# Seven-phase fp32 network: norm sums on VectorE, the norm's factor spread by a product with the identity, gate product and some weight parts on VectorE

## The chip, the cores and the metric

The kernel runs on one core of one Trainium2 chip. The metric is the device time of one execution in microseconds; lower is better. The reference's inputs are 512 tokens of width 1024 (and 256 memory tokens), everything in fp32.

## The reference, cut to what matters

Seven residual phases follow each other. Each starts with a root-mean-square norm, whose sum runs over the 1024 features of a token:

```
rmsnorm(x, g) = x * rsqrt(mean(x*x, axis=-1) + eps) * g
h  = x + mixer(rmsnorm(x))                 # mix: gated state-space part (inner norm "ssd") and pooling part
h += memory_attention(rmsnorm(h), rmsnorm(mem))   # xattn: 4 heads, 256 memory tokens
h += (silu(gate) * up) @ w_down            # ffn: gate, up = rmsnorm(h) @ w_gate_up, 2 x 2816 wide
h  = rmsnorm(h)                            # end of the first block ("end")
h += stick_breaking_attention(rmsnorm(h))  # stick ("begin"): 16 heads
h += relu(rmsnorm(h) @ w1)**2 @ w2         # mlp1: 4096 wide
h += nsa_attention(rmsnorm(h))             # nsa: compressed, selected and window attention, shared K and V
h += relu(rmsnorm(h) @ w1)**2 @ w2         # mlp2
out = rmsnorm(h)                           # "final"
```

## The kernel before, in words

**Layout.** Activations lie feature-major: `h` is 8 k-tiles of 128 features by 512 tokens. A projection yields one 128x512 PSUM bank per output tile, a *group*. fp32 products are put together from two parts of each operand, a rounded high part and the remainder: `group` (L556) issues, for each k-tile, the matmuls `wh*xh`, `wh*xl`, `wl*xh`. So a group over eight k-tiles is 24 matmuls of 128x128 weights by 512 tokens, one over six k-tiles 18.

**Weights.** `Weights` (L303) goes through one list of pieces (mostly 128x1024) in the order of use. For each piece, SP loads it into `ws` (3 buffers), ScalarE copies the rounded part `wh` (L341), and the remainder `wl` = `ws` - `wh` is a subtraction (L350): on GpSimd for the 14 pieces named in the set `POOL_LO` (L29), on VectorE for all others. `get` (L363) makes pieces two ahead of the one that it returns, inside the instruction stream of whatever asks for it; `no0`, the attention's output projection, asks for three ahead (L2003). Pieces of the second projection in feed-forward's last block are 768 wide (six k-tiles).

**Norms.** `Norm.tile` (L382) is called for each of the eight k-tiles as it becomes final. ScalarE squares it (L385 for the first, straight into `acc`; L388 into `sq`, two buffers, for the others), and GpSimd adds the square into `acc` (L392, seven times a norm, six for "final", half the width for the memory). `ssq` (L426) is a product with a column of ones that brings the token sums onto partitions, and a few small VectorE and ScalarE instructions (L412) that give the factor `tm`, 128 tokens by 4 columns. `bcast` (L429) spreads this factor over all 128 partitions: for each of the four columns VectorE multiplies the identity by the column (`dg`, two buffers, L436), TensorE multiplies a matrix of ones by it (L437), and VectorE copies the 128x512 result out of PSUM (`r`, L439). `Norm2` (L444), between the two blocks, keeps two norms, "end" and "begin", fed from the same tiles, and spreads two factors.

**Who calls them.** `proj` (L565) runs three lead groups, the sums (`ssq`), a fourth group, then `bcast`, and evacuates the groups with the spread factor afterwards. Evacuations of the mixer's pooling projection, `ev_pool` (L811), place the sums and broadcasts of "ssd" (m = 4, 5) and of the memory (m = 6, 7) between groups, behind VectorE's addition into `h` (L812). `feed` (L631) is the end of a residual phase: VectorE adds the group to `h` (L628), then `Norm.tile`, then the split into `xh` on ScalarE (L552) and `xl` on VectorE (L553) for the next phase; weight remainders of the next groups come between tiles. At the end of feed-forward (L1311 on) `ev` does this for eight tiles and feeds both norms of `Norm2`. `g_z` (L787) gates the mixer's output tile by tile and feeds the norm "ssd" in the midst of the state-space work. In feed-forward's first projections `ev` (L1279) scales each group by the factor (L1281); for even groups ScalarE takes the Silu (L1283), for odd ones GpSimd multiplies by the gate (L1286, 22 times), and the product is split.

**Order.** The scheduling is manual: each engine runs its instructions in the order in which the program issues them, so an instruction that waits holds all later ones of its engine. SP issues the weight loads, ScalarE some others. Generators in `bg` are advanced by `tick` between groups.

Of the kernel before, what the change touches and what calls it, by code (L numbers as in the profile page):

```python
# [10 lines left out]
F32 = mybir.dt.float32  # L11
# [3 lines left out]
ALU = mybir.AluOpType  # L15
# [3 lines left out]
P = 128  # L19
# [6 lines left out]
NEG = -1e30  # L26
CMP_FIRST = {1: (0,), 2: (1,), 3: (2, 3)}
CMP_AT = (1, 2, 4, 5)
POOL_LO = {"xs3", "xs5", "C1", "v1", "v4", "v6", "v7", "mk3", "xq6", "nc01", "nk10", "cw0.1", "nq3",  # L29
           "no3"}  # L30
PHASES = ("mix", "xattn", "ffn", "stick", "mlp1", "nsa", "mlp2")
BANKS = {"b": range(8), "bp": [0], "bo": [1], "za": [2, 3], "zb": [4, 6],
         "s": [0, 1, 2], "t": [3, 4, 5, 6], "av": [7], "f": [0, 1, 2, 3]}
# [269 lines left out]
class Weights:  # L303
# [42 lines left out]
    def lo(self):  # L346
        while self.half:
            i, s, n, hi, lo = self.half.popleft()
            e = self.nc.gpsimd if self.pieces[i][0] in POOL_LO else self.nc.vector
            e.tensor_tensor(lo[:, :n], s, hi[:, :n].bitcast(F32), op=ALU.subtract)  # L350
# [20 lines left out]
class Norm:  # L371
# [10 lines left out]
    def tile(self, src, scale=1.0):  # L382
        nc = self.s.nc
        if self.count == 0:
            nc.scalar.activation(self.acc, src, AF.Square, scale=scale)  # L385
        else:
            q = self.s.keep.tile([P, T], F32, name=f"sq_{self.name}{self.count}", tag="sq", bufs=2)
            nc.scalar.activation(q[:, :self.n], src, AF.Square, scale=scale)  # L388
            if self.count == KT - 1 and self.apart:
                self.rest = q  # L390
            else:
                nc.gpsimd.tensor_tensor(self.acc, self.acc, q[:, :self.n], op=ALU.add)  # L392
        self.count += 1

    def mean(self, src=None, more=None):
# [33 lines left out]
    def bcast(self, tm=None, tag="rbc", bufs=2):  # L429

        s, nc = self.s, self.s.nc
        tm = self.tm if tm is None else tm
        ps = s.bank()
        for i in range(self.n // P):
            dg = s.keep.tile([P, P], F32, name=f"dg_{self.name}{i}", tag="dg", bufs=2)
            nc.vector.tensor_scalar(dg, s.ident, tm[:, i:i + 1], None, op0=ALU.mult)  # L436
            nc.tensor.matmul(ps[:, P * i:P * i + P], s.ones, dg, start=True, stop=True)  # L437
        r = s.keep.tile([P, T], F32, name=f"r_{self.name}", tag=tag, bufs=bufs)[:, :self.n]
        nc.vector.tensor_copy(r, ps[:, :self.n])  # L439
        self.bc = r  # L440
        return r
# [26 lines left out]
class Kernel:  # L468
# [799 lines left out]
    def _ffn(self):  # L1268
        nc = self.nc
        norm, (xh, xl) = self.norm, self.x  # L1270
        hid = [self.newx(), (self.tmp("hh", (P, KT, T), F32R, bufs=1),
                             self.tmp("hl", (P, KT, T), F32R, bufs=1))]
        gate = {}

        def up(b, norm_):
            j0, j1 = FF_BLOCKS[b]
            hh, hl = hid[b % 2]

            def ev(i, ps):  # L1279
                t = self.tmp("t", bufs=4)  # L1280
                nc.vector.tensor_tensor(t, ps, norm.bc, op=ALU.mult)  # L1281
                if i % 2 == 0:
                    nc.scalar.activation(t, t, AF.Silu)  # L1283
                    gate[0] = t
                else:
                    nc.gpsimd.tensor_tensor(t, t, gate[0], op=ALU.mult)  # L1286
                    self.split(hh[:, i // 2, :], hl[:, i // 2, :], t)

            self.proj([f"f{a}{j}" for j in range(j0, j1) for a in "gu"], xh, xl, ev, norm=norm_)

        def down(b, ev):
            j0, j1 = FF_BLOCKS[b]
            self.proj([f"fd{b}.{m}" for m in range(8)], *hid[b % 2], ev, nk=j1 - j0)

        def plain(m, ps):
            nc.vector.tensor_tensor(self.h[:, m, :], self.h[:, m, :], ps, op=ALU.add)

        up(0, norm)
        up(1, None)
        down(0, plain)  # L1300
        up(2, None)
        down(1, plain)
        if self.nxt == "stick":
            nxt, nx = Norm2(self), self.newx()
            gf = self.col("final_norm")
            both = self.keep.tile([P, KT], F32, name="gboth")
            nc.vector.tensor_tensor(both, gf, self.next_gain, op=ALU.mult)
            nc.scalar.preload_act_table_set("natural_log_exp_and_others")

            def ev(m, ps):  # L1310
                self.resid(m, ps, nxt, both, nx)  # L1311
                nxt.second.tile(self.h[:, m, :], gf[:, m:m + 1])
        else:
            nxt, nx = None, None

            def ev(m, ps):
                plain(m, ps)
        down(2, ev)
        self.norm, self.x = nxt, nx
# [899 lines left out]
```

## Time and profile before

| | |
|---|---|
| median of three runs | 2227.06 us (2223.79 to 2227.17) |
| the profiled execution | 2227.83 us |
| its span, first to last instruction | 2226.0 us |
| mean granted TensorE clock | 0.990 |
| VectorE, ScalarE busy in the span | 55%, 39% |

The profile is that of one execution. A time in a row is microseconds unless marked ns; a stretch A:B counts from the span's start. Busy times are summed per engine; "PE" is TensorE's matmuls, "PEld" its weight loads, DVE is VectorE, ACT is ScalarE, POOL is GpSimd. An instruction is named by its line in the kernel, its engine, its operation and the tiles it writes and reads. An arrow (`<-DVE wl L350`) names what the engine waited for: the idle time before the instruction ended when that one did.

### The profile page before, as it was taken

The page shows a single profiled execution, that of the slowest core. Times are in us where ns is not written, and L with a number is a line of the kernel's source. Part 1 is how long each engine was busy: PE and PEld are TensorE (multiplying, and loading weights), DVE is VectorE, ACT ScalarE, POOL GpSimd, SP SyncE. Part 2 cuts the span into 40 slices and gives each one's busy share as a digit, 9 for nine tenths or more (in the row PEclk, how much of TensorE's full clock was granted, in tenths as well). Part 3 has the DMA queues.
Part 4 walks back from the last instruction along what each step waited for, and adds up shares of the span by engine and source line. Part 5 has one row for each costly group of instructions (what it writes and reads, how often), then busy time and mean ns, then how long its engine had stood idle before and what let it go on. Part 6 is the DMA issues. An engine that isn't in the chain of part 4 may idle for free.

```text
span 2226.0 us, 26742 instructions
## 1 busy us (share of the span) xinstructions
PE 2141.3 (96%) x10250; PEld 1735.1 (78%) x10250; DVE 1217.6 (55%) x1965; ACT 875.5 (39%) x1405; POOL 410.2 (18%) x429
## 2 busy tenths in 40 slices
PE   8899999999999999999899999999988899999998
PEld 5687888888888887877678888888766668888886
DVE  6988656554333336567655343445767745534333
ACT  4334434343222224355534332334547643523222
POOL 3433401011110104122210000012137631000001
PEclk9999999999999999999999999999999999999999
DMA  4222434122333223322132333324330113333231
GB/s 139 69 66 82 142 106 152 57 75 94 97 102 96 95 84 106 114 76 67 57 115 94 104 95 95 102 88 133 127 100 22 30 43 119 105 95 104 95 95 66
DMA packets 63375, 205.93 MB, mean 93 GB/s; under 512 B 7952, under 2 KB 8336, under 8 KB 63120
## 3 DMA queue, kind: packets, MB, share of 16 engines
q1 hardware_dynamic: 59504, 196.86, 28.2%
q10 hardware_dynamic: 3744, 7.37, 0.9%
q8 instruction: 80, 1.31, 0.2%
q14 instruction: 47, 0.39, 0.1%
HBM read 189.39 MB, written 6.29 MB: 88 GB/s over the span
## 4 chain that ended last, share of the span: by engine, by line
PE 77%; DVE 11%; ACT 5%; POOL 3%; issue 3%; DMA 1%; ACTq 0%; SPq 0%; POOLq 0%; DVEq 0%
PE psum L540 60%; PE b L540 15%; DVE wl L350 2%; POOL sph L1685 1%; ACT sT L1667 1%; ACT sT L1668 1%; PE psum L2092 1%; DVE t L908 1%; DVE spl L1690 1%; DVE xl L553 1%; DVE np L2070 1%; DVE sT L1662 1%; ACT xh L552 1%; DMA nq<-nq 1%; DVE pv L1089 0%
## 5 line engine op out<-in xcount | busy, mean ns | idle before, releaser
L540 PE MATMUL psum<-xh,wh 128*128 128x512 f32 x1560 | 610.8, 392 | 1.6 <-DVE h L628 0.9
L540 PE MATMUL psum<-xh,wl 128*128 128x512 f32 x1560 | 608.4, 390 | 3.2 <-DVE wl L350 3.0
L540 PE MATMUL psum<-xl,wh 128*128 128x512 f32 x1560 | 607.8, 390 | 0.0
L341 ACT ACTIVATE wh<-ws 128x1024 fp32r<-128x1024 f32 (+1 forms) x346 | 356.5, 1038 | 376.5 <-PE psum L540 312.8
L350 DVE TENSOR_TENSOR wl<-ws,wh 128x1024 fp32r<-128x1024 f32 (+2 forms) x332 | 415.6, 1257 | 90.3 <-ACT wh L341 90.2
L540 PEld LDWEIGHTS psum<-xh,wl 128*128 128x128 f32 x1560 | 292.6, 188 | 67.7 <-DVE wl L350 5.8
L540 PEld LDWEIGHTS psum<-xh,wh 128*128 128x128 f32 x1560 | 292.7, 188 | 63.8 <-issue 2.8
L540 PEld LDWEIGHTS psum<-xl,wh 128*128 128x128 f32 x1560 | 292.7, 188 | 60.3
L540 PE MATMUL b<-xh,wh 128*128 128x512 f32 (+1 forms) x488 | 194.5, 399 | 6.5 <-ACT wh L341 6.5
L540 PE MATMUL b<-xh,wl 128*128 128x512 f32 (+1 forms) x488 | 192.3, 394 | 3.8 <-POOL wl L350 1.9
L540 PE MATMUL b<-xl,wh 128*128 128x512 f32 (+1 forms) x488 | 192.1, 394 | 0.5 <-DVE xl L553 0.5
L540 PE MATMUL psum<-hh,wh 128*128 128x512 f32 x320 | 125.1, 391 | 0.0
L540 PE MATMUL psum<-hh,wl 128*128 128x512 f32 x320 | 124.6, 389 | 0.0
L540 PE MATMUL psum<-hl,wh 128*128 128x512 f32 x320 | 124.6, 389 | 0.0
L1356 DVE TENSOR_TENSOR h<-h,psum 128x512 f32<-128x512 f32 x48 | 33.0, 688 | 161.2 <-PE psum L540 161.2
L1347 ACT ACTIVATE t<-t 128x512 f32<-128x512 f32 x64 | 40.5, 632 | 188.8 <-DVE t L1346 188.8
L540 PEld LDWEIGHTS b<-xh,wh 128*128 128x128 f32 (+1 forms) x488 | 92.1, 189 | 26.0 <-ACT wh L341 6.5
L540 PEld LDWEIGHTS b<-xh,wl 128*128 128x128 f32 (+1 forms) x488 | 91.8, 188 | 26.1 <-DVE wl L350 3.3
L553 DVE SCALAR_TENSOR_TENSOR xl<-h,cols,xh 128x512 fp32r<-128x512 f32 x64 | 76.0, 1202 | 66.0 <-ACT xh L552 66.0
L540 PEld LDWEIGHTS b<-xl,wh 128*128 128x128 f32 (+1 forms) x488 | 92.1, 189 | 20.3 <-DVE xl L553 1.2
L540 PE MATMUL psum<-ks,nq 128*128 128x256 f32 (+2 forms) x256 | 72.5, 377 | 15.9 <-DVE nmx L2070 9.2
L2084 POOL TENSOR_SCALAR np<-np,nsm,gates 128x512 f32<-128x512 f32 (+3 forms) x128 | 80.3, 633 | 39.5 <-PE psum L2092 22.3
(497 smaller groups left out, 3055.2 us busy)
## 6 DMA issues: line engine op xcount, KB each, us to landing
ws<-in_wst SPq DMA_DIRECT2D x332, 512.0 KB, 3.4
h<-in_xT SPq DMA_DIRECT2D x16, 256.0 KB, 3.5
kk<-kk SPq DMA_DIRECT2D x16, 256.0 KB, 3.6
nq<-nq SPq DMA_DIRECT2D x16, 256.0 KB, 2.9
ws<-in_wst SPq DMA_DIRECT2D x8, 384.0 KB, 3.1
spill<-back SPq DMA_DIRECT2D x8, 256.0 KB, 2.8
back<-spill ACTq DMA_DIRECT2D x8, 256.0 KB, 3.4
spill<-h ACTq DMA_DIRECT2D x8, 256.0 KB, 6.0
```

Of the source, the lines that this page charges most:

```text
L341: self.nc.scalar.activation(hi[:, :n], s, AF.Copy)
L350: e.tensor_tensor(lo[:, :n], s, hi[:, :n].bitcast(F32), op=ALU.subtract)
L540: self.nc.tensor.matmul(ps, a, b, start=start, stop=stop, skip_group_check=again)
L552: nc.scalar.activation(hi, src, AF.Copy, scale=scale)
L553: nc.vector.scalar_tensor_tensor(lo, src, scale, hi.bitcast(F32), op0=ALU.mult, op1=ALU.subtract)
L908: nc.vector.scalar_tensor_tensor(t, u[:, q:q + T], cw[:, q:q + 1], t, op0=ALU.mult, op1=ALU.add)
L1347: nc.scalar.activation(t, t, AF.Square)
L1356: nc.vector.tensor_tensor(self.h[:, m, :], self.h[:, m, :], ps, op=ALU.add)
L1662: self.nc.vector.tensor_scalar(tb, zb[:, :, :384], 30.0, None, op0=ALU.min)
L1667: self.nc.scalar.activation(t, t, AF.Exp)
L1668: self.nc.scalar.activation(t, t, AF.Ln, bias=1.0)
L2084: self.nc.gpsimd.tensor_scalar(u["p"], u["p"], u.pop("sm"), self.gates[:, u["c"], e:e + 1], op0=ALU.mult, op1=ALU.mult)
```

## The change

Four edits. The set `POOL_LO` loses seven of its 14 names, so these weight remainders are made by VectorE. The additions of squares into `acc` are issued to VectorE. `bcast` no longer makes `dg`: the stationary operand of its matmul is now one column of the factor, repeated along 128 columns by the access pattern, and the moving operand is the identity. The gate product of feed-forward is issued to VectorE. Shapes, order in the program, buffers and results are otherwise the same.

```
-POOL_LO = {"xs3", "xs5", "C1", "v1", "v4", "v6", "v7", "mk3", "xq6", "nc01", "nk10", "cw0.1", "nq3",
-           "no3"}
+POOL_LO = {"xs3", "xs5", "C1", "v1", "v4", "v6", "v7"}
...
             if self.count == KT - 1 and self.apart:
                 self.rest = q
             else:
-                nc.gpsimd.tensor_tensor(self.acc, self.acc, q[:, :self.n], op=ALU.add)
+                nc.vector.tensor_tensor(self.acc, self.acc, q[:, :self.n], op=ALU.add)
...
         for i in range(self.n // P):
-            dg = s.keep.tile([P, P], F32, name=f"dg_{self.name}{i}", tag="dg", bufs=2)
-            nc.vector.tensor_scalar(dg, s.ident, tm[:, i:i + 1], None, op0=ALU.mult)
-            nc.tensor.matmul(ps[:, P * i:P * i + P], s.ones, dg, start=True, stop=True)
+            nc.tensor.matmul(ps[:, P * i:P * i + P], tm[:, i:i + 1].to_broadcast([P, P]), s.ident,
+                             start=True, stop=True)
...
                 else:
-                    nc.gpsimd.tensor_tensor(t, t, gate[0], op=ALU.mult)
+                    nc.vector.tensor_tensor(t, t, gate[0], op=ALU.mult)
                     self.split(hh[:, i // 2, :], hl[:, i // 2, :], t)
```

## Rows read from the trace of the kernel before

**Rows 1.** The page: busy times by engine, and the chain that ended last.
```profile
PE 2141.3 (96%) x10250; PEld 1735.1 (78%) x10250; DVE 1217.6 (55%) x1965; ACT 875.5 (39%) x1405; POOL 410.2 (18%) x429
...
PE 77%; DVE 11%; ACT 5%; POOL 3%; issue 3%; DMA 1%; ACTq 0%; SPq 0%; POOLq 0%; DVEq 0%
```

**Rows 2.** Busy by stretch: length, engines, granted clock, DMA share, GB/s.
```profile
115.00:225.00 110.00, 106.15 (x558) 85.14 (x557) 94.70 (x163) 39.54 (x65) 40.93 (x32) 1.00 0.23 74
520.00:835.00 315.00, 314.84 (x1395) 260.73 (x1395) 124.12 (x152) 87.83 (x107) 28.40 (x22) 1.00 0.30 95
873.80:877.20 3.40, 3.40 (x9) 2.65 (x9) 3.28 (x2) 1.65 (x3) 3.40 (x3) 0.50 0.24 95
```

**Rows 3.** Groups by line and form: count | busy, mean ns | idle before, releaser.
```profile
L350 DVE TENSOR_TENSOR wl<-ws,wh 128x1024 fp32r<-128x1024 f32 x318 | 397.0, 1253 | 90.3 <-ACT wh L341 90.2
L1101 DVE TENSOR_TENSOR pdl<-t,pdh 128x512 fp32r<-128x512 f32 x8 | 5.5, 687 | 2.9 <-ACT pdh L1098 2.9
...
L392 POOL TENSOR_TENSOR acc_ffn<-acc_ffn,sq_ffn 128x512 f32<-128x512 f32 x7 | 9.0, 1290 | 80.5 <-ACT sq_ffn L388 80.5
L1286 POOL TENSOR_TENSOR t<-t,t 128x512 f32<-128x512 f32 x22 | 28.4, 1291 | 257.3 <-DVE t L1281 232.8 <-ACT t L1283 24.5
```

**Rows 4.** Line 437 on TensorE: instructions; idle before them by releaser (us, times).
```profile
L437 PE MATMUL b<-dg_ssd,ones x8: 275/275/377, 278.7 to 280.0; 128*128 128x128 f32 x8
...
DVE dg_end L436: 1.1, 2
...
DVE dg_mem L436: 1.0, 1
DVE dg_mlp L436: 0.3, 2
...
DVE dg_ffn L436: 0.2, 1
```

**Rows 5.** Timeline of VectorE, feed-forward's end: start, duration, instruction, idle before, releaser.
```profile
838.75 0.95 DVE L350 TENSOR_TENSOR wl<-ws,wh 128x768 fp32r<-128x768 f32 x1
...
845.33 0.68 DVE L628 TENSOR_TENSOR h<-h,psum 128x512 f32<-128x512 f32 x1
847.37 1.28 DVE L553 SCALAR_TENSOR_TENSOR xl<-h,gboth,xh 128x512 fp32r<-128x512 f32 x1 [1.37 <-ACT xh L552]
848.57 2.04 DVE L350 TENSOR_TENSOR wl<-ws,wh 128x768 fp32r<-128x768 f32 x1
850.54 0.68 DVE L628 TENSOR_TENSOR h<-h,psum 128x512 f32<-128x512 f32 x1
```

**Rows 6.** Timeline of GpSimd, the same stretch.
```profile
846.81 1.29 POOL L392 TENSOR_TENSOR acc_end<-acc_end,sq_end 128x512 f32<-128x512 f32 x1 [2.22 <-ACT sq_end L388]
```

**Rows 7.** Timeline of TensorE, the same stretch.
```profile
866.58 0.50 PE L540 MATMUL psum<-wl,xh 128*128 128x512 f32 x1 [1.11 <-DVE wl L350]
...
868.07 0.39 PE L540 MATMUL psum<-wl,xh 128*128 128x512 f32 x1
872.60 0.50 PE L540 MATMUL psum<-wh,xh 128*128 128x512 f32 x1 [4.15 <-DVE h L628]
```

**Rows 8.** Timeline of the start: VectorE and TensorE.
```profile
10.98 2.29 DVE L350 TENSOR_TENSOR wl<-ws,wh 128x1024 fp32r<-128x1024 f32 x1
...
13.32 0.80 PE L540 MATMUL b<-xh,wl 128*128 128x512 f32 x1 [1.82 <-DVE wl L350]
```

**Rows 9.** Timeline of TensorE, the end of stick.
```profile
1161.13 0.50 PE L540 MATMUL psum<-xh,wl 128*128 128x512 f32 x1 [1.54 <-DVE wl L350]
```

**Rows 10.** Timeline of GpSimd and TensorE, the end of nsa.
```profile
1807.75 2.36 POOL L350 TENSOR_TENSOR wl<-ws,wh 128x1024 fp32r<-128x1024 f32 x1 [1.62 <-ACT wh L341]
...
1810.91 0.55 PE L2092 MATMUL psum<-small,np 128*128 128x128 f32 x3 [1.59 <-POOL np L2084]
```

**Rows 11.** Timeline of VectorE and GpSimd in the mixer's z stage.
```profile
211.12 0.73 DVE L1074 SCALAR_TENSOR_TENSOR h<-h,cols,b 128x512 f32<-128x512 f32 x1
...
211.94 1.29 POOL L392 TENSOR_TENSOR acc_ssd<-acc_ssd,sq_ssd 128x512 f32<-128x512 f32 x1 [1.29 <-ACT sq_ssd L388]
```

## The prediction

> **What bounds the kernel now.** I read the page's busy shares first: TensorE is busy for 2141.3 of 2226.0 us, VectorE for 1217.6, GpSimd for 410.2. The chain that ended last is 77% TensorE, 11% VectorE and only 3% GpSimd [rows 1]. So TensorE sets the time nearly everywhere; an edit is worth something only where TensorE stands still, or where it makes TensorE stand still. Next I read the busy time by stage. Feed-forward (520 to 835) is full: 314.84 of 315 us, and 315 / 1395 gives 0.226 us from one matmul to the next. The mixer's z stage (115 to 225) has VectorE at 94.70 of 110 and TensorE idle for 3.85 [rows 2]. Last I looked at the idle times of TensorE one by one, and at what released each; the rest of the argument is at those places.
>
> Two facts price the change. An elementwise 128x512 operation with two SBUF inputs costs 0.687 on VectorE and 1.29 on GpSimd [rows 3]. And the engines slow each other: at the feed-forward's end a 768-wide weight remainder takes 0.95 on VectorE with GpSimd quiet (838.75), and 2.04 when a GpSimd addition lies beside it (848.57, addition from 846.81) [rows 5, 6]. So GpSimd work that lies beside VectorE is paid twice, and moving it costs VectorE less than its price says.
>
> **The change part by part.**
>
> *Broadcast.* Per norm, four (memory: two) VectorE products with the identity go, and with them what TensorE waits for. Its idle time on these: 1.1 at end, as much at the gated norm of the mixer (ssd, built alike), 1.0 at mem, 0.3 at the two mlp norms together, 0.2 each at ffn and four more of the same kind (in, xattn, begin, nsa) [rows 4]: 1.1 + 1.1 + 1.0 + 0.3 + 5 x 0.2 = 4.5. A wait costs more than its idle time: from 868.07 to 872.60 are 4.53, less a step of 0.226 is 4.30, against 4.15 shown as idle [rows 7], so 0.15 more each. There are 12 (three long ones, nine between the second and third product, as two buffers serve four): 1.8. The factor itself is ready long before, as ssq comes one group earlier. Gain 6.3 (4.5 to 6.3). Matmul count and shape stay; the new stationary operand is one column repeated over 128, which no row shows at this place: taken at nothing, the other end is rival C.
>
> *The feed-forward's end*, where seven tiles feed two norms (14 additions) while stick's first weights are made. VectorE's period per tile is 5.21 (845.33 to 850.54) [rows 5]; TensorE needs 18 steps of 0.226 = 4.07 for its group of six k, so the deficit grows until it stalls 1.11 and 4.15 [rows 7], with restarts 5.56. After the change the period is made of: 1.48 from h's start until the square is there (846.81 - 845.33 [rows 5, 6]), addition 0.69, xl (today 1.28 stretched; nearest alone 0.69), second addition 0.69, remainder 0.95: 4.50. Neighbours overlap by 0.08 (847.37 + 1.28 against 848.57), four times: 4.2. Two of the last remainders are 1024 wide, 1.253 each [rows 3]: 4.5. Over some six periods VectorE gains about 1.0 each, 6.0, more than the stall: I take 5.5 (3 to 5.6, as the new additions stand in VectorE's in-order queue behind ScalarE's square, and xl, the remainder and the next h behind them). After that stall TensorE had a stretch at half clock: 9 matmuls in 3.40 us at a granted 0.50, that is 1.2 GHz [rows 2]; at 0.226 they need 2.03. It follows the stall, so I let it go with it: 1.4 (0 to 1.4). Sum 6.9.
>
> *Start.* TensorE idles 1.82 for C0's remainder, which took 2.29 on VectorE [rows 8] against a mean of 1.253 [rows 3]. Without GpSimd's additions beside it this remainder alone gives back 1.04, the two xl ahead of it more, and one or two additions of 0.69 come into the queue before it. I take 1.5 (0 to 1.8).
>
> *Stick to mlp1.* The seven additions of the mlp norm move. TensorE idles 1.54 for a remainder [rows 9], plus 0.15; same pattern as above with one addition. I take 1.7 (0 to 2.0).
>
> *Weight parts.* Of the seven remainders that move, no3 matters: on GpSimd it lies from 1807.75 for 2.36 in front of the scaling that TensorE then waits 1.59 for [rows 10]. Its going gives 1.74 with the restart; but on VectorE it waits for its ScalarE half with the attention's work queued behind it. I take 1.3 (0 to 1.74). The other six (mk3, xq6, nc01, nk10, cw0.1, nq3) each add 1.253 to VectorE in stretches where TensorE's idle times have other releasers: 0; without that cover 6 x 1.25 = 7.5.
>
> *Gate.* 22 products of 1.29 [rows 3] become 22 x 0.69 = 15.2 of VectorE in a stage where it works 124.12 of 315 us [rows 2], and TensorE is never idle. Behind a product wait the next evacuations, and eight PSUM banks cover them: 0. If the cover failed, at most 15.2.
>
> *z stage.* Here VectorE is nearly full. It must now wait for ScalarE's square before each of seven additions: at 211.12 it went straight on, while the square released GpSimd only at 211.94 [rows 11]. So a wait of 0.82 and 0.69 of work, less overlap 1.4 per tile; against it GpSimd's additions no longer stretch its neighbours, and GpSimd is freed of 1.29 per tile. I take a loss of 0.8 (gain 2 to loss 9.8).
>
> *Other norms* (xattn, mem, ffn, nsa, mlp2, final): additions in stretches where VectorE has gaps and TensorE's waits are on something else: 0.
>
> Sum: 6.3 + 6.9 + 1.5 + 1.7 + 1.3 - 0.8 = 16.9. The profiled execution took 2227.83, so 2210.9; that execution lies 0.77 above the median of 2227.06, which makes 2210.2.
>
> The Trainium skill speaks against the direction ("Perfetto Trace Analysis", "Optimizing Scalar/DVE Operations"): where VectorE is saturated, offloading to ScalarE or even GpSimd can pay, though it adds that between the two that share the port it may not help. Over the span VectorE is at 55%, in the z stage at 86% [rows 1, 2]: by the rule's first half that stage and the ends of the blocks would lose (rival D), by its second half they need not.
>
> **Rivals.**
>
> B, another wait takes the place at the ends of feed-forward and stick. For it: each addition now hangs on ScalarE, which squares twice and splits per tile. Against: ScalarE releases GpSimd's addition 1.48 after h [rows 5, 6], far inside 4.07. Then 6.9 and 1.7 are lost: 2210.2 + 8.6 = 2218.8.
>
> C, the repeated column is slow to load: the weight load then does not hide. TensorE issues the four products of a norm as eight instructions [rows 4], so 76 for the 38 products of all norms; a load is 260.73 / 1395 = 0.187 [rows 2]. Each fully exposed: 76 x 0.187 = 14.2, so 2224.4, and most of what the change does is gone. Against: loads hide beside matmuls everywhere else.
>
> D, slower: VectorE's queue. One mechanism, the wait for the square at the head of an in-order queue, with no relief of the neighbours. The end of feed-forward then loses 14 x 0.69 = 9.7 instead of gaining 6.9, stick to mlp1 loses 7 x 0.69 = 4.8 instead of 1.7 gained, the z stage loses 7 x 1.4 = 9.8 instead of 0.8: 2210.2 + 16.6 + 6.5 + 9.0 = 2242.3. It decides where VectorE's period at feed-forward's end stays above 5.21. For it: the order on VectorE is the program's. Against: remainder and xl lose 1.09 and some 0.6 today to exactly the work that goes [rows 3, 5].
>
> **Numbers.** A, as forecast, 0.70, with 2204 (bounds at the good ends, 5 to 6 less) to 2217 (feed-forward's end at 3, start, clock and no3 at 0) as its own range; B 0.17; C 0.06; D 0.07. The range runs from 2201, beyond A's end for half-clock stretches that may also go after no3, to 2222, past B and short of C and D. This kernel tells 0.2% (4.5 us) from no change. Faster: A, and B (8.3 below), less a little: 0.86. Same: C and part of B: 0.07. Slower: D: 0.07.
>
> **What would show it.** Right: no idle time of TensorE ahead of the broadcasts; at feed-forward's end a period of VectorE near 4.2 to 4.5, remainders of 768 at 0.95, xl under 0.8, no stall near 868 to 872 and full clock after it; start's wait below 0.5. Wrong: remainders still near 2, or additions that show long waits for squares with the next h late (B, D); the broadcast matmuls further apart than before (C); more than 5 us of idle TensorE between 115 and 225 (D). The forecast fails if feed-forward's end or the broadcasts give back less than half.

## The result, and the profile after

The changed kernel takes 2207.65 us (median of four runs, 2205.24 to 2209.69) against 2227.11 for the kernel before: a ratio of 0.9916, interval 0.99 to 0.9931. That is 19.5 us less; 16.9 were forecast, and the forecast time was 2210.2. The four runs lie on two levels, two near 2205.4 and two at 2209.69, and the median falls between them. The profiled execution, on the lower level, took 2205.24, its span is 2203.5 and its mean granted clock 0.993.

The page's busy times and chain, in the same columns as [rows 1]:

```profile
PE 2130.0 (97%) x10250; PEld 1730.3 (79%) x10250; DVE 1231.0 (56%) x2032; ACT 876.1 (40%) x1405; POOL 261.2 (12%) x324
...
PE 78%; DVE 10%; ACT 4%; POOL 4%; issue 3%; DMA 1%; SPq 0%; ACTq 0%; POOLq 0%; DVEq 0%
```

GpSimd lost 149 us of work, and VectorE's busy time rose by 13 only (1217.6 to 1231.0). Priced one by one, the moved operations would have added some 65: 76 additions and 22 products at 0.69 (seven of half the width at 0.42), and seven remainders at 1.25, less 38 products with the identity at some 0.25. What is missing from the 65 is time that VectorE no longer loses beside GpSimd. The experiments below, each with one of the edits, show where. With the sums alone (first line) VectorE is busy for 4.2 more than the 1217.6 of before, where its additions price at 50.5; with the gate alone (second line) it has 15.0 more, of 15.2 priced. So nearly all of the relief is at the sums, some 5 at the remainders (3.8 in place of 8.8), and none at the gate.

```profile
PE 2135.4 (97%) x10250; PEld 1732.1 (78%) x10250; DVE 1221.8 (55%) x2041; ACT 875.5 (40%) x1405; POOL 305.9 (14%) x353
PE 2143.6 (96%) x10250; PEld 1736.8 (78%) x10250; DVE 1232.6 (55%) x1987; ACT 875.4 (39%) x1405; POOL 381.9 (17%) x407
```

**At the broadcasts.** Line 434 of the changed kernel on TensorE (instructions; its list of idle times is empty where [rows 4] has the waits):

```profile
L434 PE MATMUL b<-small,y_ssd x8: 271/275/275, 276.6 to 277.4; 128*128 128x128 f32 x8
...
its engine sat idle before it (us, times) until:
who waited for it (us, times):
```

and its timeline around the broadcast of ffn (start, duration, instruction):

```profile
520.01 0.39 PE L538 MATMUL psum<-xh,wl 128*128 128x512 f32 x1
520.24 1.05 PE L434 MATMUL psum<-small,y_ffn 128*128 128x128 f32 x8
521.04 0.48 PE L538 MATMUL psum<-xh,wh 128*128 128x512 f32 x1
```

Eight instructions in 0.80 us (521.04 - 520.24), 0.10 each, without a gap; the kernel before took 1.23 for its eight here (525.79 to 527.02). The repeated column shows no cost against the stored matrix of ones: its weight loads have a median of 190 ns, those of the matrix 188.

**At the end of feed-forward.** VectorE's timeline, one tile, to be held against [rows 5]. In the kernel before a second addition of GpSimd, which the rows there do not show, lay beside the remainder of 848.57; its line stands first, the changed kernel's timeline after it:

```profile
848.06 1.74 POOL L392 TENSOR_TENSOR acc_begin<-acc_begin,sq_begin 128x512 f32<-128x512 f32 x1
```

```profile
838.31 0.68 DVE L626 TENSOR_TENSOR h<-h,psum 128x512 f32<-128x512 f32 x1
839.75 0.69 DVE L391 TENSOR_TENSOR acc_end<-acc_end,sq_end 128x512 f32<-128x512 f32 x1 [0.76 <-ACT sq_end L387]
840.37 0.75 DVE L551 SCALAR_TENSOR_TENSOR xl<-h,gboth,xh 128x512 fp32r<-128x512 f32 x1
841.03 0.68 DVE L391 TENSOR_TENSOR acc_begin<-acc_begin,sq_begin 128x512 f32<-128x512 f32 x1
841.64 0.95 DVE L349 TENSOR_TENSOR wl<-ws,wh 128x768 fp32r<-128x768 f32 x1
842.51 0.68 DVE L626 TENSOR_TENSOR h<-h,psum 128x512 f32<-128x512 f32 x1
```

The period is 842.51 - 838.31 = 4.20; before it was 5.21. VectorE has two operations more per tile and is done a microsecond sooner. The first addition and its wait of 0.76 for the square lie in the time for which VectorE stood before xl already (1.37 in [rows 5]); the second waits for nothing. And xl went from 1.28 to 0.75, the remainder from 2.04 to 0.95. TensorE's busy time over this stretch (columns as in [rows 2]) in the changed kernel:

```profile
800.00:870.00 70.00, 70.00 (x310) 57.71 (x309) 38.64 (x52) 28.96 (x40) 2.37 (x6) 1.00 0.35 104
```

TensorE is busy for all of 70 us; the stalls of 1.11 and 4.15 [rows 7] are gone.

**Stage by stage.** TensorE runs the same 10250 matmul instructions in the same order in every version here, so the time from the start of one numbered matmul to that of another can be held against each other. This table is worked out from the records of five profiled executions; three of them are experiments told below. Stretches left out (160 to 716, 734 to 940) differ by under 0.4 between the columns.

```
matmuls          what lies there                    before  changed  spread    sums  remainders
   0 to 30       start                               13.74    11.11   13.67   10.66     14.39
  30 to 160      broadcast of in                     28.03    27.60   27.60   28.05     28.03
 716 to 734 and 940 to 1030  z stage                 20.69    22.66   20.73   22.62     20.72
1030 to 1975     broadcasts of ssd, mem, xattn      192.20   189.09  188.86  192.25    192.44
1975 to 2005     xattn's scores                       5.37     3.88    3.88    5.37      3.88
2005 to 3900     feed-forward, broadcast of ffn     422.41   421.96  421.93  422.37    422.40
3900 to 3990     end of feed-forward                 28.25    20.61   28.23   20.59     28.24
3990 to 4305     broadcasts of begin, end            68.70    66.58   66.58   68.68     68.68
4305 to 5100     stick                              160.03   160.18  159.80  159.77    159.79
5100 to 5380     end of stick                        62.87    60.25   62.90   60.25     62.60
5380 to 7140     mlp1, broadcasts of mlp, nsa       395.96   395.38  395.10  395.97    396.19
7140 to 7160     nsa, remainder nk10                  4.04     4.97    4.05    4.01      4.97
7160 to 8400     nsa attention                      234.98   233.52  234.83  234.97    233.30
8400 to 8470     end of nsa, remainder no3           16.05    13.20   14.47   14.49     13.18
8470 to last     mlp2, broadcast of mlp             395.94   395.57  395.52  395.93    395.94
```

The gains of the broadcasts and of the sums are plain in it, and two losses, the z stage and nk10. Part of what moves is the TensorE clock and not TensorE's waits: xattn's scores, nsa's attention and 1.6 of the end of nsa, told after the last run. The start differs by up to 2.4 us between profiles with the same code there.

### The profile page after: what moved, and what is told of

Read it like the earlier page. It is cut to its first block, busy times and chain, and to the rows that moved or that the text cites. A ratio compares the mean times of both kernels' runs of the same rounds, so it can differ in the third digit from the quotient of the medians.

```text
span 2203.5 us, 26617 instructions
## 1 busy us (share of the span) xinstructions
PE 2130.0 (97%) x10250; PEld 1730.3 (79%) x10250; DVE 1231.0 (56%) x2032; ACT 876.1 (40%) x1405; POOL 261.2 (12%) x324
## 4 chain that ended last, share of the span: by engine, by line
PE 78%; DVE 10%; ACT 4%; POOL 4%; issue 3%; DMA 1%; SPq 0%; ACTq 0%; POOLq 0%; DVEq 0%
PE psum L538 62%; PE b L538 14%; POOL sph L1683 1%; DVE wl L349 1%; ACT sT L1665 1%; ACT sT L1666 1%; DVE t L906 1%; PE psum L2090 1%; DVE spl L1688 1%; DVE sT L1660 1%; DVE np L2068 1%; DMA nq<-nq 1%; DVE pv L1087 0%; DVE sT L1659 0%; POOL np L2082 0%
## 5 line engine op out<-in xcount | busy, mean ns | idle before, releaser
L1344 DVE SCALAR_TENSOR_TENSOR t<-psum,r_mlp 128x512 f32<-128x512 f32 x64 | 44.2, 690 | 79.1 <-PE psum L538 79.0
```

The costliest lines, as they stand in the source:

```text
L1344: nc.vector.scalar_tensor_tensor(t, ps, 0.0, norm.bc, op0=ALU.max, op1=ALU.mult)
```

## The experiments

Theory: the gains sit at separate places of the trace and add up, and where GpSimd's additions went, the gain is that VectorE is no longer stretched. Rivals: the parts need each other; half-clock stretches carry the sum; what held feed-forward's end was the chain of sums on GpSimd and its buffers, not the contention.

**Each part alone** (each from the kernel before, on one chip, where that kernel took 2226.67).

The broadcast:

```
-            dg = s.keep.tile([P, P], F32, ...
-            nc.vector.tensor_scalar(dg, s.ident, tm[:, i:i + 1], None, op0=ALU.mult)
-            nc.tensor.matmul(..., s.ones, dg, start=True, stop=True)
+            nc.tensor.matmul(..., tm[:, i:i + 1].to_broadcast([P, P]), s.ident, ...
```

> The kernel before with the broadcast edit alone. Theory (the parts sit at separate places and add up): TensorE's waits on the identity products go, three of 1.13 us and nine of about 0.43, so 7.3 us less than before (6 to 8.5), about 2219.8; the 76 broadcast instructions stand no further apart than before. Rival (the parts need each other, the broadcast waits being only VectorE's lateness from other work): under 3 us less. Rival of the slow load of a repeated column: 0 or slower, with gaps of some 0.19 between the broadcast instructions.

Measured 2218.68 (2216.52 to 2220.74), ratio 0.9966 (0.9952 to 0.9979): 8.0 less.

The sums:

```
-                nc.gpsimd.tensor_tensor(self.acc, self.acc, q[:, :self.n], op=ALU.add)
+                nc.vector.tensor_tensor(self.acc, self.acc, q[:, :self.n], op=ALU.add)
```

> The kernel before with the additions of squares alone moved to VectorE. Theory: start 2.2 less, feed-forward's end 7.4 less (VectorE's period there 4.2), end of stick 2.2 less, z stage 1.8 more: 10 us less in sum (7 to 12), about 2217. Rival (the parts need each other: without the relief of the broadcast the additions crowd VectorE): under 5 us less, or slower. Rival (stretches at half clock come and go by chance and carry the sum): the places named differ by under half of these figures, and the time moves in steps of about 1.4.

Measured 2214.63 (2214.0 to 2216.32), ratio 0.9947 (0.9934 to 0.9959): 12.0 less. In the table the end of feed-forward is 20.59 against 28.25, the end of stick 60.25 against 62.87, the z stage 22.62 against 20.69: the very figures of the changed kernel, without the other parts.

The remainders:

```
-POOL_LO = {"xs3", ..., "v7", "mk3", "xq6", "nc01", "nk10", "cw0.1", "nq3", "no3"}
+POOL_LO = {"xs3", ..., "v7"}
```

> The kernel before with the seven weight remainders alone moved to VectorE. Theory: no3 gives back 2.0 to 3.1 at the end of nsa, nk10 costs 1.2 in nsa's compression (VectorE has it behind other work), the other five nothing: 0.8 to 2 us less, about 2225.5. Rival (all seven are hidden): no change within 0.5. Rival (they crowd VectorE): 2 us or more slower.

Measured 2224.7 (2223.13 to 2227.31), ratio 0.9993 (0.9984 to 1.0002): 2.0 less, within the interval of no change. In the table nk10 costs 0.93 and the end of nsa is 2.87 shorter, of which half is not its doing; nsa's attention is 1.68 shorter, which seems to go with nk10 (both below).

The gate:

```
-                    nc.gpsimd.tensor_tensor(t, t, gate[0], op=ALU.mult)
+                    nc.vector.tensor_tensor(t, t, gate[0], op=ALU.mult)
```

> The kernel before with the gate products of feed-forward alone moved to VectorE. Theory: TensorE is never idle in that stage, VectorE has 40% more than half of its time free: no change, within 1 us of before, and TensorE busy for over 314.5 of 315 us between 520 and 835. Rival (a wait of the evacuations behind the product): up to 15 us slower.

Measured 2226.21 (2225.21 to 2227.59), ratio 1.0001 (0.9992 to 1.001): nothing. Its busy times in the stretch of [rows 2]:

```profile
520.00:835.00 315.00, 314.84 (x1398) 260.84 (x1397) 139.94 (x174) 87.83 (x107) 0.00 (x0) 1.00 0.33 95
```

VectorE has 15.8 us more to do (139.94 against 124.12), GpSimd nothing, and TensorE's 314.84 is the same to the last digit.

8.0 + 12.0 + 2.0 + 0.5 make 22.5, against 19.5 for all four together: the parts add up within what the intervals allow (each single ratio is good to 2 to 3 us), and none is seen to need another.

**Contention put back.** The changed kernel with an addition on GpSimd that nobody reads, beside each addition on VectorE at feed-forward's end, with four buffers for the squares there in place of two, so that the added reads hold nobody up; and, from the kernel before, the four buffers alone. The lines of the addition:

```
+                if self.name in ("end", "begin"):
+                    j = self.s.ph.tile([P, T], F32, ..., tag="jk", bufs=2)
+                    nc.gpsimd.tensor_tensor(j, q, self.s.h[:, self.count, :], op=ALU.add)
```

> The changed kernel with an addition on GpSimd beside each of VectorE's additions at feed-forward's end, into a tile that nobody reads; it adds work and takes nothing away, and the squares of these two norms have four buffers, so that the added reads hold nobody up. Theory (what the change gives there is that VectorE is no longer stretched by GpSimd): the 768-wide remainder goes back from 0.95 to about 2, xl from 0.75 to about 1.3, VectorE's period from 4.2 to 5.5 or more, and the stall comes back: 7 to 16 us slower than the changed kernel. Rival (what held the kernel before was the length of the chain of sums on GpSimd and its two square buffers): no change within 1 us, as nothing waits for the added operations.

Measured 2223.05 (2219.13 to 2224.05), ratio to before 0.9979 (0.9971 to 0.9988): 15.4 slower than the changed kernel. By matmul number the end of feed-forward (3900 to 3990) takes 35.38 against 20.61, so 14.8 lie at this one place. VectorE's timeline of that run, and then GpSimd's:

```profile
844.86 0.67 DVE L632 TENSOR_TENSOR h<-h,psum 128x512 f32<-128x512 f32 x1
846.23 0.69 DVE L394 TENSOR_TENSOR acc_end<-acc_end,sq_end 128x512 f32<-128x512 f32 x1 [0.70 <-ACT sq_end L390]
846.85 1.78 DVE L557 SCALAR_TENSOR_TENSOR xl<-h,gboth,xh 128x512 fp32r<-128x512 f32 x1
848.55 1.78 DVE L394 TENSOR_TENSOR acc_begin<-acc_begin,sq_begin 128x512 f32<-128x512 f32 x1
850.25 0.94 DVE L349 TENSOR_TENSOR wl<-ws,wh 128x768 fp32r<-128x768 f32 x1
851.12 0.67 DVE L632 TENSOR_TENSOR h<-h,psum 128x512 f32<-128x512 f32 x1
```

```profile
846.34 1.74 POOL L397 TENSOR_TENSOR jk_end<-sq_end,h 128x512 f32<-128x512 f32 x1 [2.83 <-ACT sq_end L390]
848.04 1.74 POOL L397 TENSOR_TENSOR jk_begin<-sq_begin,h 128x512 f32<-128x512 f32 x1
```

The period is 851.12 - 844.86 = 6.26, though nothing waits for GpSimd. The expectation had the wrong instructions: the remainder keeps its 0.94, since GpSimd is done by 849.78; xl and the second addition, which now lie beside GpSimd, take 1.78 each in place of 0.75 and 0.68, so 2.1 more, which is the whole of 6.26 - 4.20. xl ends 0.55 after the GpSimd operation (848.63 and 848.08), so it seems to have run only when that one was over. The Trainium skill says so ("SBUF — State Buffer", "SBUF: two separate sides") for a VectorE operation with two SBUF inputs beside a GpSimd one that reads SBUF: the pair of ports that the two engines share goes as an exclusive lock to whichever operation starts first, and the other blocks fully; these rows agree, to within the 0.2 by which 0.55 is short of xl's own 0.75. By that rule a GpSimd operation can cost VectorE up to its own length; here 1.74 of it cost 1.0 to 1.1. TensorE's waits came back, larger than in [rows 7]:

```profile
PE psum L544 <- DVE h L632: 5.0, 1, 5.0
PE psum L544 <- DVE wl L349: 4.5, 3, 2.2
```

The buffers:

> The kernel before with four buffers instead of two for the squares of the two norms at feed-forward's end. Theory (VectorE is stretched by GpSimd's additions): no change within 1 us, VectorE's period there stays near 5.2. Rival (ScalarE's squares, and with them xh and xl, wait until GpSimd has read the buffers): up to 7 us less than before, period near 4.2.

Measured 2226.26 (2224.96 to 2227.28), ratio 0.9999 (0.9991 to 1.0008). VectorE's period there is still 5.21, with xl and remainder stretched as before:

```profile
844.42 0.68 DVE L631 TENSOR_TENSOR h<-h,psum 128x512 f32<-128x512 f32 x1
846.41 1.33 DVE L556 SCALAR_TENSOR_TENSOR xl<-h,gboth,xh 128x512 fp32r<-128x512 f32 x1 [1.31 <-ACT xh L555]
847.66 2.05 DVE L350 TENSOR_TENSOR wl<-ws,wh 128x768 fp32r<-128x768 f32 x1
849.63 0.67 DVE L631 TENSOR_TENSOR h<-h,psum 128x512 f32<-128x512 f32 x1
```

So the two buffers did not hold the kernel before; and the run above was slow with no chain of sums on GpSimd at all. That rival is out.

**The two losses taken back.** The z stage first: in the changed kernel VectorE stands idle before ssd's addition, and TensorE later waits longer for the decayed scores (`d`) than before. VectorE's and TensorE's timelines:

```profile
209.02 0.69 DVE L391 TENSOR_TENSOR acc_ssd<-acc_ssd,sq_ssd 128x512 f32<-128x512 f32 x1 [0.70 <-ACT sq_ssd L387]
```

```profile
213.19 0.43 PE L538 MATMUL b<-d,xc 128*64 128x128 f32 x2 [1.77 <-POOL d L1052]
```

At the same matmul TensorE was idle for less in the kernel before:

```profile
215.48 0.43 PE L540 MATMUL b<-d,xc 128*64 128x128 f32 x2 [1.14 <-POOL d L1054]
```

The wait itself is only 0.63 longer. The changed kernel's clock then fell (1.2 GHz, columns as in [rows 2]), and the matmuls up to the next group took 3.81 (214.42 to 218.23) where the kernel before took 2.38 (216.71 to 219.09):

```profile
215.60:218.40 2.80, 2.80 (x14) 2.76 (x14) 2.52 (x2) 0.77 (x2) 1.79 (x1) 0.50 0.22 32
```

The edit puts the seven additions of this norm back:

```
+                e = nc.gpsimd if self.name == "ssd" else nc.vector
+                e.tensor_tensor(self.acc, self.acc, q[:, :self.n], op=ALU.add)
```

> The changed kernel with the additions of the one norm ssd (gated mixer output) back on GpSimd. Theory: the wait for the square at the head of VectorE's queue goes from the z stage, so the 1.8 us that the changed kernel lost between 213 and 220 come back: 1.8 less than the changed kernel (0.5 to 2.5). Rival (the loss there is a stretch at half clock that has nothing to do with the additions): no change, or the stretch stays.

Measured 2203.34 (2201.16 to 2203.99), ratio to before 0.9893 (0.9879 to 0.9906): 4.3 below the changed kernel's median, where 1.8 (0.5 to 2.5) were expected, and 2.0 below its lower level. Its z stage takes 20.73, as before the change.

Then the remainder. VectorE and TensorE in the changed kernel:

```profile
1545.88 1.41 DVE L1452 TENSOR_TENSOR ks<-nkr,ks 64x512 fp32r<-64x512 f32 x2
1547.32 1.23 DVE L349 TENSOR_TENSOR wl<-ws,wh 128x1024 fp32r<-128x1024 f32 x1
```

```profile
1548.60 0.50 PE L538 MATMUL psum<-wl,xh 128*128 128x512 f32 x1 [0.69 <-DVE wl L349]
```

```
-POOL_LO = {"xs3", "xs5", "C1", "v1", "v4", "v6", "v7"}
+POOL_LO = {"xs3", "xs5", "C1", "v1", "v4", "v6", "v7", "nk10"}
```

> The changed kernel with the weight remainder nk10 back on GpSimd. Theory: TensorE's wait of 0.69 (0.86 lost) for it near 1548 goes and the two after it stay as before: 1.2 us less than the changed kernel. Rival (GpSimd takes 2.66 us for it beside VectorE's xl, which lie behind): the loss turns up at the next wait, within 0.4 of the changed kernel.

Measured 2208.66 (2202.76 to 2209.55), ratio 0.9913 (0.9899 to 0.9926): no lower time. In its trace the stretch 7140 to 7160 is 4.09 against 4.97, so the 0.9 is there. But nsa's attention, the stretch behind it, takes 234.90 against 233.52, so 1.4 are lost again: the rival that the loss turns up elsewhere came true, though not at the next wait (see the rows that moved, below). Its profile also lies on the upper of the two levels, with a z stage of 25.19. One of its five runs, at 2202.76, lies below all of the changed kernel's; no trace of it was kept. Both together, and the changed kernel again, on one chip (before 2227.68):

> The changed kernel with the additions of the norm ssd and the remainder nk10 both back on GpSimd. Theory: the two losses of the change go at two separate places, 1.9 or more in the z stage and 1.0 in nsa's compression: 3 to 5.5 us less than the changed kernel, 23 to 25 less than before. Rival (nk10's gain is lost at the next wait, as its run alone showed no lower time): the same as with ssd alone back, within 0.5.

> The changed kernel once more, for a comparison on the same chip as the two others. Theory: its executions fall on two levels some 4 us apart, near 2205.4 and 2209.6, and the z stage makes 2.5 of that step (22.7 us for the stretch of matmuls 716 to 734 and 940 to 1030 at the lower level, 25.2 at the upper). Rival: the two levels come from half-clock stretches elsewhere alone, with the z stage the same in both.

Both back: 2204.83 (2203.96 to 2205.89), ratio 0.99 (0.9886 to 0.9913). The changed kernel again: 2205.38, its four runs 2205.28, 2205.36, 2205.4 and 2209.04; so the two levels are there, but the advantage of taking both back is 0.5 on this chip's medians, not 3 to 5.5. Nk10's return brought no gain here either: the version without it (2203.34, on another chip) was no slower, and nsa's attention went from its 233.51 to 236.73. The profile of the changed kernel fell on the upper level this time (2209.04). Its z stage takes 25.21, against 22.66 in the profile of 2205.24: 2.55 of the 3.80 between them. Both have a stretch at half clock there, one tile apart. TensorE's timeline there:

```profile
223.62 0.43 PE L538 MATMUL b<-d,xc 128*64 128x128 f32 x2 [1.19 <-POOL d L1052]
225.82 1.23 PE L538 MATMUL b<-d,xc 128*64 128x128 f32 x14 [1.77 <-POOL d L1052]
```

One tile on, `d` is late for 1.19 and 1.77, where the profile at the lower level has a single short wait:

```profile
224.93 1.09 PE L538 MATMUL b<-d,xc 128*64 128x128 f32 x14 [0.46 <-POOL d L1052]
```

The profiles of both versions with ssd's additions back show 20.73, so these additions, with the half clock behind the wait, are what costs 1.9 or 4.5 there. What makes an execution fall on one level or the other was not found out.

**Why the additions cost in the z stage.** Two versions with nk10 back keep ssd's additions on VectorE, one tile late:

```
+                if self.name == "ssd":
+                    self.held()          # adds the square of the tile before
+                    self.hold = q
```

> The changed kernel with nk10 back on GpSimd and with ssd's additions still on VectorE, but each issued one tile later, when its square is long done. Theory (what costs in the z stage is the wait for ScalarE's square at the head of VectorE's queue, 0.70 a tile): no wait at these additions, and the z stage within 0.5 of the run with both back. Rival (the 0.69 of work itself, on a VectorE that is busy for 86% there): TensorE's waits there stay as in the changed kernel, 1.9 or more above before.

Measured 2209.96 (2209.43 to 2211.68), ratio 0.9926 (0.9913 to 0.994). The z stage takes 20.49, a little less than with the additions on GpSimd: the work of 0.68 costs nothing there, the wait for the square was the price. But the total is 4.6 above the changed kernel's on the same chip. The stretch 1030 to 1975 has 4.3 of it, 193.36 against 189.08; what the z stage gained went in nsa's attention, 237.66 against 233.44, as with the other versions with nk10 back. VectorE and TensorE:

```profile
269.28 0.68 DVE L821 TENSOR_TENSOR h<-h,b 128x512 f32<-128x512 f32 x1
269.88 0.68 DVE L401 TENSOR_TENSOR acc_ssd<-acc_ssd,sq_ssd 128x512 f32<-128x512 f32 x1
```

```profile
270.62 1.05 PE L412 MATMUL b<-ones,acc_ssd 128*128 128x1 f32 x8 [2.39 <-DVE acc_ssd L401]
```

The last addition was issued only with the sums, behind an addition into h that itself waits for TensorE; TensorE idled 2.39 for it, and a stretch at half clock came after (granted clock 0.74 from 271.5 to 278.0). So the last version issues the last addition at once:

```
                     self.hold = q
+                    if self.count == KT - 1:
+                        self.held()
```

> As the run with ssd's additions one tile late, but the last addition is issued at once with the one before it, and not at the sums. Theory (the late version lost its gain because its last addition stood in VectorE's queue behind an addition into h that waits for a group of TensorE, 2.39 us of wait and a stretch at half clock behind it): the stretch of matmuls 1030 to 1975 goes from 193.4 back to 189.1 and the z stage (716 to 734 and 940 to 1030) stays near 20.6: 3.5 to 5 us less than the late version, near 2205. Rival (the z stage's gain only hides until the next wait): time as the late version, within 1.

Measured 2203.04 (2202.1 to 2204.21), ratio 0.9896 (0.988 to 0.9913). The stretch 1030 to 1975 is back at 189.08 and the z stage at 20.49. That is 4.3 of the 6.9 below the late version, as expected; 2.7 more are nsa's attention, 234.94 against 237.66, which this edit does not touch. VectorE's timeline in the z stage has no wait at the addition:

```profile
215.17 1.78 DVE L806 SCALAR_TENSOR_TENSOR h<-pv,t 128x512 f32<-128x512 f32 x1
216.88 0.68 DVE L403 TENSOR_TENSOR acc_ssd<-acc_ssd,sq_ssd 128x512 f32<-128x512 f32 x1
217.48 0.73 DVE L1085 SCALAR_TENSOR_TENSOR h<-h,cols,b 128x512 f32<-128x512 f32 x1
```

It and the version with only ssd's additions back (2203.34) are the fastest, some 4 us below the changed kernel's first median and 2 below its second (2205.38). The intervals of the ratios overlap, though every execution of the two (2201.16 to 2204.21) lies below every one of the changed kernel's eight (2205.24 to 2209.69).

**The rows that moved without an edit.** In xattn's scores the same 30 matmuls take 5.37 or 3.88. The kernel before, then the changed one (columns as in [rows 2]):

```profile
423.60:426.70 3.10, 3.10 (x16) 3.10 (x16) 2.40 (x5) 1.60 (x3) 0.00 (x0) 0.51 0.53 169
```

```profile
418.50:421.00 2.50, 2.50 (x23) 2.50 (x22) 1.80 (x3) 1.12 (x3) 0.00 (x0) 1.00 0.26 46
```

The granted clock is 0.51 in one and 1.00 in the other: 1.2 GHz and 2.4. But the gate's run has 3.88 there and the changed kernel's second profile 5.40, so this is not the change's. Likewise about 1.57 of the end of nsa, which the spread and sums runs lost too (14.47 and 14.49 against 16.05) without touching it.

The nsa attention (7160 to 8400) is another matter. All five profiles with nk10's remainder on VectorE have 233.3 to 233.5 there, all nine with it on GpSimd 234.8 to 237.7. Two pairs differ in nothing but nk10: 233.52 (changed kernel) and 234.90 (nk10 back), 233.51 (ssd back) and 236.73 (both back). Most of it lies between matmuls 7540 and 7620 (the sums' run is fast there and loses its 1.7 later, from 8300 to 8320); the same stretch in the kernel before and in the changed one:

```profile
1650.50:1670.80 20.30, 16.99 (x80) 10.94 (x81) 12.22 (x51) 11.93 (x38) 14.49 (x22) 0.79 0.12 27
1632.70:1651.40 18.70, 15.53 (x81) 10.88 (x81) 12.29 (x52) 12.02 (x38) 14.58 (x22) 0.84 0.13 29
```

The granted clock is higher in the second. So nk10's move, which costs 0.93 at its own place, seems to give back 1.4 or more here, and its return takes that away; why the clock follows it stays open. Of the 22.6 between the two profiled executions 1.49 + 1.57 = 3.1 come and go without an edit, and 1.46 go with nk10.

## Why the prediction was right, point by point

- **Broadcast**: forecast 6.3; the stretches that hold them give 0.43 + 3.11 + 0.45 + 2.12 + 0.58 + 0.37 = 7.1, and the part alone 8.0 in time. Right, a little short: a short wait cost 0.43, since eight instructions take 0.80 now and 1.23 before, where idle 0.2 and restart 0.15 had been counted. Rival C is out.
- **Feed-forward's end**: forecast 6.9 with a period of 4.2; measured 7.6 and 4.20, half clock after it gone. Rival B, and D here, are out: the first addition of a tile does wait 0.76 for its square, as B had it, but inside the period, and the second not at all. One reading was wrong without harm to the sum: GpSimd's addition from 846.81 ends at 848.10, so it lies beside xl; beside the remainder of 848.57 lies the second addition, from 848.06.
- **Start**: forecast 1.5; the stretch is 2.63 shorter, but its size is not well known: with the additions on GpSimd the profiles have 12.50 to 14.88 there, with them on VectorE 10.08 to 12.47. TensorE's wait for C0's remainder is 0.25 in place of 1.82; the remainder takes 1.22 in place of 2.29. In the run with four buffers it took 1.21, and the wait was 0.59, with the additions still on GpSimd, so the stretching there hangs on where they fall. The changed kernel:

```profile
10.26 1.22 DVE L349 TENSOR_TENSOR wl<-ws,wh 128x1024 fp32r<-128x1024 f32 x1
...
11.53 0.79 PE L538 MATMUL b<-xh,wl 128*128 128x512 f32 x1 [0.25 <-DVE wl L349]
```

- **Stick to mlp1**: forecast 1.7; the stretch is 2.62 shorter, in the sums' run too, and no wait for a remainder is left. The rest beyond the 1.7 was not forecast; some of it is two smaller waits of TensorE, 0.8 (now 0.5) and 0.2 (gone).
- **no3**: forecast 1.3; the stretch lost 2.85, 1.57 of it clock that also went elsewhere, so 1.3. VectorE did wait for its ScalarE half, 0.50 only, with TensorE's wait at 0.51:

```profile
1788.36 1.23 DVE L349 TENSOR_TENSOR wl<-ws,wh 128x1024 fp32r<-128x1024 f32 x1 [0.50 <-ACT wh L340]
...
1790.92 0.76 PE L2090 MATMUL psum<-small,np 128*128 128x128 f32 x4 [0.51 <-POOL np L2082]
```

- **The other six remainders**: forecast 0, with 1.25 each where the cover fails. It fails for nk10: 0.93 lost at its place, though nsa's attention got 1.4 or more faster with it. This step was wrong: the remainder stands on VectorE behind two operations into `ks` (from 1545.88), and is begun at 1547.32 only, when TensorE is about to need it.
- **Gate**: forecast 0, measured 0. That VectorE was not relieved there has a plain reason in the trace of the kernel before: it stood idle beside all 22 products of GpSimd. The one at 560.87 to 562.16, for instance, lies between VectorE's operations ending at 560.70 and starting at 562.86.
- **z stage**: forecast a loss of 0.8 (gain 2 to loss 9.8); measured 1.9 or 4.5. This term was mis-sized, and the 0.8 was a choice within its range, worked out from no rows: the wait of 0.70 stands on the path to `d`, on which TensorE waits, and the half clock behind such a wait, 1.4 at the lower level, was not in the sum. What GpSimd gained by the lighter load was worth little, 0.2 (20.49 against 20.73). The Trainium skill's rule that a saturated VectorE may be relieved by offloading to GpSimd ("Perfetto Trace Analysis", "Optimizing Scalar/DVE Operations") pointed the right way for this stage, with 1.9 or more; but the late versions show that it was the wait and not the load.

The mechanism held at the places that carry the sum. That the total came within 2.6 us is in part luck: terms that were too small (broadcast, feed-forward, start, stick: 0.8 + 0.7 + 1.1 + 0.9) stand against the z stage (1.1 to 3.7 too kind), and clock that comes and goes adds 3 in the profile.

## What to carry to other kernels

An elementwise operation on GpSimd can be paid on both engines, where VectorE works on SBUF inputs beside it: before pricing a move to VectorE, take off what its neighbours lose today; here 149 us of GpSimd work became 13 of VectorE. Look for the neighbours first: the gate's products had none, and cost VectorE their full price. What a move can cost is not its duration but its place in an in-order queue: issue an operation that waits for another engine one tile late, yet never so late that it stands behind an instruction which waits for the engine that needs it. Hold stages against each other by matmul number, since stretches at half clock, worth some 1.5 us each here, come and go between executions of one kernel.

## What the runs showed that was not expected

- At feed-forward's end a VectorE operation on SBUF inputs (xl, the addition) that starts while a GpSimd one with two SBUF inputs runs took 1.78 in place of 0.68 to 0.75, and ended about 0.55 after the other did.
- One column of 128 values, repeated 128 times by the access pattern, serves as stationary operand at 0.10 us an instruction, with no loss seen against the stored matrix of ones.
- The changed kernel has two levels 4 us apart, and 2.55 of that is one more late tile in the z stage, not the clock alone.
- Moving one weight remainder (nk10) went with a shorter time at half clock some 85 us later, worth more than the move cost; the cause is open.
